# A two-layer hybrid decoder step: pooling gates with their branch products in the attention rounds, the other gates earlier, and a new order inside projections

## The chip, the cores and the metric

The program runs on one core of one Trainium2 chip. The metric is device time in microseconds (us), the median of several executions. Engines are called by the profile's names: PE (TensorE, matmuls), DVE (VectorE), ACT (ScalarE), POOL (GpSimd) and SP (SyncE, which only issues transfers).

## What is computed

Each of two layers takes 256 prompt tokens and 64 sample tokens (8 sequences of 8) of width 1024 through one input projection and three parallel mixers, and merges them under gates:

```
h = xn @ w_in        # pooling input and z, q, kv, rope key, z, conv q/k/v, z, beta, alpha, 3 x 1024 gates
y_a = pool_mixer(h_pool) * silu(z_pool)          # trailing windows of 2, 4, 8, 16
y_b = latent_attention(h_q, h_kv, h_kr) * silu(z_mla)   # samples attend to 2048 cached positions
y_c = rmsnorm(gated_delta(short_conv(h_qkv))) * silu(z_dn)
gates = sigmoid(h_gate)                          # three of 1024
merged = gates[0] * (y_a @ w_br_pool) + gates[1] * (y_b @ w_br_mla) + gates[2] * (y_c @ w_br_dn)
x = x + merged @ w_out
```

After both layers a last RMSNorm is applied. Caches and states are outputs too.

## The kernel before, in words

All activations stand transposed: 128 channels on the partitions, 320 tokens (256 and 64) along them. The width of 1024 makes eight such tiles, and a column block of a weight is a tile of 128 x 1024 (eight blocks of k).

**Products.** Every weight is loaded by SP (`load_w`, four buffers `wraw`) and split in two parts for accuracy: `split_w` has ACT write the rounded part `wh` (line 200) and DVE the rest `wl` (line 201). The numbers in K["lo"] name the splits of a layer whose second part POOL makes instead of DVE. `mm3` (line 213) multiplies with the parts of the activations: for each of eight k, wh by xnH (line 224), wh by xnL (line 225) and wl by xnH (line 226), 24 matmuls into one PSUM bank. A branch product has four k and so 12 matmuls. The first two products of the first layer use another order, both wh products of all k and then all wl products (lines 219 to 221).

**Stages of a layer.** Conv units (`unit`, `value`: a projection, its eviction into V at lines 500 and 501, three steps `cy` at line 509, a gate function) alternate with chunk products of the delta rule; poolings, z projections and latents are fillers that `fill` takes from a list, in the order of K["fo"] and in the numbers that other entries of K give. Then come the inverse of the chunk matrices, the state steps over chunks, eight prompt heads, eight decode rounds (one for each sample sequence, with 2048 cached keys gathered from memory) and the tail: branch products, the merged sum and eight output products. Up to the heads and in the tail a list scheduler puts the instructions of all engines in order; from the heads to the first branch products the order is the program's own (`manual_schedule`) for PE, DVE, ACT and POOL.

**Gates.** There are 24 gate products in a layer, named (n, m): n = 0 for pooling, 1 for the delta rule, 2 for attention, and m one of eight tiles. `gate_w` takes the next of the list `order` and splits its weight, `gate_mm` multiplies, `gate_out` has DVE multiply the bank with the norm (line 464) and ACT take the tanh. Eight (first layer) or seven stand in stages before the heads and stay in SBUF (`early`, 11 buffers `gt`), two among the heads, two in each of six rounds and one in the last two; those 14 are written to memory by ACT's queue and read back in the tail by POOL's. One gate of the second layer stands in the tail.

**A round.** Scores (72 matmuls of four row groups), the largest score and exponent on DVE and ACT, a gate, the combination of the sequence before (`olat`), the first half of the second gate, the turning of the exponents (`PT`, on PE), the other half, and the weighted sum (`pv`). DVE transposes the next keys meanwhile (`flip`).

**Branch products.** `branch_mm` multiplies; `branch_out` multiplies with the gate on DVE (for n = 0 straight into the sum `acc`, line 1358; else line 1360) and has POOL add into the sum (line 1361). In the last round and behind it stand two of the pooling's, two of the delta rule's, then one and two more; the rest follow in the scheduled part. PSUM's four banks "A" serve all of them.

Of the kernel before, what the change touches and what calls it, by code (L numbers as in the profile page):

```python
# [11 lines left out]
F32 = mybir.dt.float32  # L12
# [22 lines left out]
NG = 11  # L35
# [5 lines left out]
KS = [{'kk': [1, 1, 2, 3], 'ga': 3, 'gm': [0, 2, 0], 'un': 16, 'gb': 0, 'gc': [0, 0, 0], 'ft': [5, 2, 3, 3, 2], 'fu': [0, 1, 2, 1], 'fn': 3, 'gs': [0, 0, 2, 1, 0], 'gq': 0, 'gp': [0, 0, 0, 0, 0, 1, 1, 0], 'ge': [1, 1, 1], 'ya': 'B', 'zb': 'A', 'fy': [2, 1, 1], 'fz': [1, 1, 1], 'p1': [2, 2, 2, 2], 'p2': [2, 2, 2, 2], 'hd': [3, 0, 2, 1, 1, 1, 0, 0], 'fo': [0, 1, 2, 3, 4, 5, 6, 7, 8, 9, 12, 13, 10, 14, 11, 18, 15, 16, 17, 19], 'to': [0, 2, 6, 1, 3, 5, 7, 13, 14, 8, 15, 16, 18, 9, 17, 10, 4, 11, 12], 'bt': ['A', 'A', 'A', 'A', 'M'], 'lo': [1, 2, 4, 5, 8, 13], 'zp': [-1, -1, -1, 19, -1, -1, -1, -1], 'f8': 3}, {'kk': [1, 1, 2, 3], 'ga': 3, 'gm': [0, 0, 0], 'un': 8, 'gb': 1, 'gc': [0, 0, 0], 'ft': [5, 2, 3, 3, 1], 'fu': [0, 1, 2, 1], 'fn': 3, 'gs': [0, 0, 2, 1, 0], 'gq': 0, 'gp': [0, 0, 0, 0, 0, 1, 1, 0], 'ge': [1, 1, 2], 'ya': 'B', 'zb': 'B', 'fy': [2, 1, 2], 'fz': [1, 0, 1], 'p1': [2, 2, 3, 1], 'p2': [2, 2, 2, 2], 'hd': [3, 0, 2, 1, 1, 1, 0, 0], 'fo': [0, 1, 5, 2, 3, 4, 6, 7, 8, 9, 12, 13, 10, 14, 11, 18, 15, 16, 17, 19], 'to': [0, 2, 5, 1, 6, 3, 7, 13, 14, 8, 15, 16, 18, 9, 17, 10, 4, 11, 12], 'bt': ['A', 'A', 'A', 'M', 'M'], 'lo': [1, 2, 4, 5, 15], 'zp': [-1, -1, -1, 19, -1, -1, -1, -1], 'f8': 3}]  # L41
LEVELS = (8, 16, 32)

GL, SPILL = (2, 2, 2, 2, 2, 2, 1, 1), 14
# [72 lines left out]
def trunk(tc, I, O, layers=2):  # L117
# [296 lines left out]
    for l in range(layers):  # L414
# [30 lines left out]
        order = [(n, 2 * mp + i) for mp in range(4) for n in range(3) for i in range(2)]  # L445
# [3 lines left out]
        spilled = {}  # L449

        def gate_w(spare=False):
            n, m = order.pop(0)
# [8 lines left out]
        def gate_out(nm, b, spill=False):  # L461

            t = per.tile([128, T], F32, tag="gs" if spill else "gt", name="gt", bufs=2 if spill else NG)
            tt(t, b[:, :T], rn, mult)
            act(t, t, AF.Tanh, scale=0.5)
            if spill:
                spilled[nm] = kept[len(spilled)]
                nc.scalar.dma_start(spilled[nm], t)
            else:
                early[nm] = t  # L470

        def gate(tag, spare=False, spill=False):
            nm, w = gate_w(spare)
            gate_out(nm, gate_mm(tag, w), spill)
# [20 lines left out]
        def conv(ct):  # L495
# [7 lines left out]
            nc.gpsimd.tensor_copy(cnew[:, ct, 0:3], V[:, 256:259])  # L503
            nc.gpsimd.tensor_copy(cnew[:, ct, 3:27].rearrange("p (b j) -> p b j", j=3), Vs[:, :, 8:])
# [30 lines left out]
        def unit(a, p):  # L535
# [6 lines left out]
            nc.gpsimd.tensor_tensor(sq, o, o, mult)  # L542
# [69 lines left out]

        unit(0, 2)
        unit(0, 3)
# [80 lines left out]
        fillers = [fillers[i] for i in K["fo"]]  # L695
        gated = [lambda p=p: zproj(8 + p, C_ZDN + 128 * p) for p in range(4)]
        gated += [lambda i=i: zproj(4 + i, C_ZMLA + 128 * i) for i in range(4)]
        for z, at in zip(gated, K["zp"]):
            if at >= 0:
                fillers.insert(at, z)  # L700
# [310 lines left out]
        fillers += [late[i] for i in K["to"] if not 5 <= i < 13 or K["zp"][i - 5] < 0]  # L1011
# [314 lines left out]
        yb = {}  # L1326

        def split_hi(pool, y0):
            yb[y0] = (pool.tile([128, 4, T], F32R, name=f"yH{y0}"), pool.tile([128, 4, T], F32R, name=f"yL{y0}"))
            for i in range(4):  # L1330
                act(yb[y0][0][:, i, :], zs[y0 + i], AF.Copy)

        def split_lo(y0):
            for i in range(4):
                tt(yb[y0][1][:, i, :], zs[y0 + i], yb[y0][0][:, i, :].bitcast(F32), sub)

        def split_y(pool, y0):
            split_hi(pool, y0)
            split_lo(y0)

# [28 lines left out]
        with tc.manual_schedule(engines={mybir.EngineType.PE, mybir.EngineType.DVE, mybir.EngineType.Activation, mybir.EngineType.Pool}):  # L1369
# [23 lines left out]
            for h in range(11):  # L1393
# [23 lines left out]
                if h == 3:  # L1417
                    gate_out(nm, b, True)
                    b = None
                if h == 8:  # L1420
                    gate_out(nm, b, True)
                    pair[0] = paired[0] = 1
                    gs = [gate_w() for _ in range(GL[0])]
# [10 lines left out]
            for bb in range(NB):  # L1434
                more = bb + 1 < NB
                if not more:
# [3 lines left out]
                    split_hi(p3a, 0)  # L1440
# [167 lines left out]
```

## Time and profile before

| what | value |
|---|---|
| median of three runs | 1044.32 us (1042.73 to 1047.79) |
| profiled execution, its time | 1044.8 us |
| its span, first to last instruction | 1042.8 us |
| mean granted clock of PE | 0.97 of full |
| busy in the span: PE, DVE, ACT, POOL | 987.6, 712.1, 466.5, 332.2 us |
| bytes read and written | 144.17 and 13.68 MB |

Busy time is the time in which an engine ran any of its instructions. Matmuls overlap in their pipeline and their ends are modelled, so PE can be busy without being at its peak; a matmul's price is read from the distance of starts. A mean over the span hides that stretches have different limits, so the rows below are cut by stretch.

### The profile page before, as it was taken

The numbers are of one execution on the slowest core, as the hardware profiler recorded it, in microseconds if no ns is written. First come the engines' busy times: TensorE is split into PE (matmuls) and PEld (weight loads), VectorE is DVE, ScalarE is ACT, GpSimd is POOL, SyncE is SP. The second block draws the span as 40 slices with busy tenths as digits, with TensorE's granted clock in tenths as the row PEclk, the third lists the DMA queues.
The fourth block names the chain that finished last, engine by engine and source line by source line (L and its number), as shares of the span: only waits on it lengthen the run. The fifth ranks groups of instructions, "written<-read, shape, count | busy, mean of one in ns | idle before, by whom it ended". The sixth has DMA issues, their size and how long they took to land.

```text
span 1042.8 us, 24809 instructions
## 1 busy us (share of the span) xinstructions
PE 987.6 (95%) x10211; PEld 865.2 (83%) x10211; DVE 712.1 (68%) x1353; ACT 466.5 (45%) x838; POOL 332.2 (32%) x467
## 2 busy tenths in 40 slices
PE   8988899999999999999989979999999999998996
PEld 6877798997878888789978868999887787877996
DVE  3899974658656666677758988646774675754962
ACT  5554253555443333444546534336455333334453
POOL 3656312124250101035445542221334201100631
PEclk8999899999999999999999989999999999999999
DMA  9533324633656776268563333455256577633861
GB/s 235 158 82 101 96 74 111 184 96 91 203 171 202 242 233 225 78 196 233 144 194 94 86 98 82 109 144 140 71 145 232 163 227 259 189 135 126 237 171 51
DMA packets 202698, 159.22 MB, mean 153 GB/s; under 512 B 27704, under 2 KB 191826, under 8 KB 200010
## 3 DMA queue, kind: packets, MB, share of 16 engines
q1 hardware_dynamic: 176364, 98.47, 34.7%
q0 software_dynamic: 7424, 48.75, 13.2%
q10 hardware_dynamic: 18798, 10.44, 3.5%
q8 instruction: 80, 1.31, 0.5%
q14 instruction: 32, 0.26, 0.1%
HBM read 144.17 MB, written 13.68 MB: 151 GB/s over the span
## 4 chain that ended last, share of the span: by engine, by line
PE 73%; DVE 16%; ACT 5%; issue 3%; DMA 2%; POOL 1%; SPq 0%; DVEq 0%; ACTq 0%; POOLq 0%
PE sc L1186 6%; PE pv L1257 6%; PE pj L224 5%; PE gate L224 5%; PE pj L226 5%; PE pj L225 5%; PE gate L226 5%; PE gate L225 4%; DVE cy L509 4%; DVE wl L201 3%; PE br L226 3%; PE br L224 3%; PE br L225 3%; PE wo L224 2%; PE wo L225 2%
## 5 line engine op out<-in xcount | busy, mean ns | idle before, releaser
L201 DVE TENSOR_TENSOR wl<-wraw,wh 128x1024 fp32r<-128x1024 f32 (+2 forms) x169 | 195.9, 1167 | 83.0 <-ACT wh L200 82.0
L200 ACT ACTIVATE wh<-wraw 128x1024 fp32r<-128x1024 f32 (+1 forms) x180 | 166.5, 935 | 156.4 <-PE pj L225 75.8
L224 PE MATMUL pj<-xnH,wh 128*128 128x320 f32 (+1 forms) x528 | 172.7, 327 | 13.0 <-DVE V L501 7.6
L226 PE MATMUL pj<-xnH,wl 128*128 128x320 f32 (+1 forms) x528 | 170.2, 322 | 6.3 <-DVE wl L201 6.0
L225 PE MATMUL pj<-xnL,wh 128*128 128x320 f32 (+1 forms) x528 | 168.6, 319 | 0.0
L224 PE MATMUL gate<-xnH,wh 128*128 128x320 f32 x384 | 125.4, 326 | 1.7 <-DVE V L501 1.5
L226 PE MATMUL gate<-xnH,wl 128*128 128x320 f32 x384 | 121.2, 316 | 2.2 <-DVE wl L201 1.8
L225 PE MATMUL gate<-xnL,wh 128*128 128x320 f32 x384 | 120.1, 313 | 0.0
L224 PEld LDWEIGHTS pj<-xnH,wh 128*128 128x128 f32 (+1 forms) x528 | 101.8, 193 | 19.0 <-ACT wh L200 7.7
L226 PEld LDWEIGHTS pj<-xnH,wl 128*128 128x128 f32 (+1 forms) x528 | 101.7, 193 | 10.6 <-DVE wl L201 7.9
L225 PEld LDWEIGHTS pj<-xnL,wh 128*128 128x128 f32 (+1 forms) x528 | 101.7, 193 | 4.9 <-issue 3.5
L224 PEld LDWEIGHTS gate<-xnH,wh 128*128 128x128 f32 x384 | 73.4, 191 | 9.3 <-issue 5.7
L1176 DVE STREAM_TRANSPOSE KT<-kv 128x1024 f32<-128x1024 f32 x64 | 78.6, 1228 | 0.5
L226 PEld LDWEIGHTS gate<-xnH,wl 128*128 128x128 f32 x384 | 73.3, 191 | 4.0 <-DVE wl L201 2.6
L225 PEld LDWEIGHTS gate<-xnL,wh 128*128 128x128 f32 x384 | 73.5, 191 | 1.1 <-issue 0.8
L224 PE MATMUL br<-yH,wh 128*128 128x320 f32 x192 | 61.1, 319 | 3.0 <-ACT wh L200 2.6
L226 PE MATMUL br<-yH,wl 128*128 128x320 f32 x192 | 60.4, 316 | 1.8 <-DVE wl L201 1.8
L225 PE MATMUL br<-yL,wh 128*128 128x320 f32 x192 | 60.2, 314 | 0.0
L1186 PE MATMUL sc<-KT,q 32*64 32x256 f32 x2048 | 59.3, 377 | 0.0
L1257 PE MATMUL pv<-kv,PT 128*64 128x256 f32 x512 | 58.8, 382 | 0.2
L509 DVE SCALAR_TENSOR_TENSOR cy<-V,prm,cy 128x344 f32<-128x344 f32 x72 | 56.4, 802 | 0.5
L1186 PEld LDWEIGHTS sc<-KT,q 32*64 32x64 f32 x2048 | 45.8, 131 | 12.0 <-issue 5.7
(410 smaller groups left out, 2045.1 us busy)
## 6 DMA issues: line engine op xcount, KB each, us to landing
wraw<-in_w_in SPq DMA_DIRECT2D x114, 512.0 KB
wraw<-in_w_out SPq DMA_DIRECT2D x16, 512.0 KB
q<-q4d SPq DMA_DIRECT2D x64, 72.0 KB
gate<-gt ACTq DMA_DIRECT2D x28, 160.0 KB
gt<-gate POOLq DMA_DIRECT2D x28, 160.0 KB, 3.5
wraw<-in_w_br_pool SPq DMA_DIRECT2D x16, 256.0 KB
wraw<-in_w_br_dn SPq DMA_DIRECT2D x16, 256.0 KB
wraw<-in_w_br_mla SPq DMA_DIRECT2D x16, 256.0 KB
```

The costliest lines, as they stand in the source:

```text
L200: act(h, raw, AF.Copy)
L201: (nc.gpsimd.tensor_tensor if spare or turn[0] in K["lo"] else tt)(lo, raw, h.bitcast(F32), sub)
L224: nc.tensor.matmul(out, wh[:, k, :], xh[:, first + k, :], start=k == 0, stop=False)
L225: nc.tensor.matmul(out, wh[:, k, :], xl[:, first + k, :], start=False, stop=False)
L226: nc.tensor.matmul(out, wl[:, k, :], xh[:, first + k, :], start=False, stop=k == nk - 1)
L509: stt(y, V[:, j : j + 344], wj(j), y, mult, add)
L1176: nc.vector.transpose(v[:, a], kv[:, a * 1024 : a * 1024 + 1024].rearrange("p (i k c) -> p i k c", i=4, k=8))
L1186: nc.tensor.matmul(sc[64 * hf : 64 * hf + 64, g, :256], q4[r, k, :], krT[r, keys_] if k == 8 else KT[r, k, keys_], start=k == 0, stop=k == 8,)
L1257: nc.tensor.matmul(pv[64 * hf : 64 * hf + 64, :256], PT[:, n * 128 + 64 * hf : n * 128 + 64 * hf + 64], kv[:, r : r + 256], start=n == 0, ...
```

## The change

Four things are done at once.

1. The eight pooling gates leave the list `order`. Round bb computes gate (0, bb) and the branch product (0, bb); the product of both, `sums[bb]`, is written to memory (`first_sum`). The splits of the pooling's activations (`split_y(p2, 0)`) go ahead of the rounds.
2. The other sixteen gates stand ahead of the rounds: 14 in stages before the heads (K["g0"], five places -1 in K["fo"] and K["gm"], K["gc"], K["gs"], K["gq"], K["ga"]), two among the heads. All are written to memory; three buffers `gs` hold them on the way. Three of the z projections move ahead in K["fo"] too.
3. `branch_out` loads the gate, and for the first product of a tile also the pooling's sum, on POOL's queue (six buffers `gt`, four `acc`). The tail has the delta rule's and the attention's products alone.
4. `mm3` takes the order "all wh products, then all wl products" wherever eight k are multiplied and no range of k is given. K["lo"] is empty: DVE makes every second part. The squares of a unit go from POOL to ACT, and ACT makes one copy of the last conv columns (`cnew`) where POOL made two.

```diff
-NG = 11
+NG = 6
-KS = [{'kk': [1, 1, 2, 3], 'ga': 3, 'gm': [0, 2, 0], 'gc': [0, 0, 0], 'gs': [0, 0, 2, 1, 0], 'gq': 0, 'lo': [1, 2, 4, 5, 8, 13],
+KS = [{'kk': [2, 1, 3, 4], 'ga': 1, 'gm': [1, 1, 0], 'gc': [0, 1, 0], 'gs': [0, 1, 1, 1, 0], 'gq': 2, 'lo': [], 'g0': [1, 1],
...
-'fo': [0, 1, 2, 3, 4, 5, 6, 7, 8, 9, 12, 13, 10, 14, 11, 18, 15, 16, 17, 19],
+'fo': [0, -1, 1, 2, -1, 3, 4, -1, 5, 6, 20, 18, 19, 7, 21, 8, 12, 9, 13, 10, 14, 11, 15, 22, 16, 17],
...
-GL, SPILL = (2, 2, 2, 2, 2, 2, 1, 1), 14
+SPILL = 16
...
     def mm3(out, w, x, nk, first=0, ks=None):
-        if l == 0 and turn[0] <= WLP:
+        if nk == 8 and not ks:
...
-        order = [(n, 2 * mp + i) for mp in range(4) for n in range(3) for i in range(2)]
+        order = [(n, 2 * mp + i) for mp in range(4) for n in (1, 2) for i in range(2)]
+        sums = [tc.dram_tile([128, T], F32, name=f"sum{l}_{m}") for m in range(8)]
...
         def gate_mm(tag, w, b=None, ks=(0, 8)):
             b = b or ps(tag, "gate")
             mm3(b[:, :T], w, xn, 8, ks=ks)
...
+        def gate_out(nm, b):
+            t = per.tile([128, T], F32, tag="gs", name="gt", bufs=3)
             tt(t, b[:, :T], rn, mult)
             act(t, t, AF.Tanh, scale=0.5)
-            if spill:
+            if nm[0]:
                 spilled[nm] = kept[len(spilled)]
                 nc.scalar.dma_start(spilled[nm], t)
...
-            nc.gpsimd.tensor_copy(cnew[:, ct, 0:3], V[:, 256:259])
-            nc.gpsimd.tensor_copy(cnew[:, ct, 3:27].rearrange("p (b j) -> p b j", j=3), Vs[:, :, 8:])
+            act(cnew[:, ct, 0:27].rearrange("p (b j) -> p b j", j=3), last3, AF.Copy)
...
-            nc.gpsimd.tensor_tensor(sq, o, o, mult)
+            act(sq, o, AF.Square)
...
         def branch_out(n, m, b):
+            t = per.tile([128, T], F32, tag="gt", name="gt", bufs=NG)
+            nc.gpsimd.dma_start(t, spilled[n, m])
+            if m not in accs:
                 accs[m] = p3a.tile([128, T], F32, tag="acc", name="acc", bufs=4)
+                nc.gpsimd.dma_start(accs[m], sums[m])
+            stt(t, t, 1.0, b[:, :T], add, mult)
+            nc.gpsimd.tensor_tensor(accs[m], accs[m], t, add)
+
+        def first_sum(m, t, b):
+            stt(t, t, 1.0, b[:, :T], add, mult)
+            nc.scalar.dma_start(sums[m], t)
...
-                g = [(gs[0][0], gate_mm("A", gs[0][1]))]
+                (nm, w), w0 = gs
+                g = gate_mm("A", w)
                 if o is not None:
                     ob = combine(o)
                     combined(bb - 1, ob)
-                if two:
-                    b = gate_mm("A", gs[1][1], ks=(0, 4))
                 PT = turned_p(S)
                 PTn = turned_own(bb)
-                    gate_mm("A", gs[1][1], b, (4, 8))
+                b = branch_mm(0, w0, "A")
                 weigh(bb, mx)
                 o = attend(bb, PT, PTn, mx)
+                first_sum(bb, t, b)
```

What the scheduler and the written order make of it is seen in the orders of instructions. Lines in the rows of the change are those of the changed file.

The first place is DVE early in the first layer, among the conv units and the decay terms (`V` is a conv eviction, `cy` a conv step, `al`, `SM`, `t1` the decays, `wl` a weight's second part, `gt` a gate). Before:

```order
L500 TENSOR_TENSOR V_475<-pj_450,rn_112 128x256
L501 TENSOR_TENSOR V_475<-pj_450,rn_112 128x8x8
L201 TENSOR_TENSOR wl_562<-wraw_559,wh_561 128x1024
L582 SCALAR_TENSOR_TENSOR al_405<-al_405,t1_406 8x320
L583 TENSOR_SCALAR al_405<-al_405,adt0_201 8x320
L585 SCALAR_TENSOR_TENSOR SM_399<-cst1_365,al_405 8x320
L500 TENSOR_TENSOR V_527<-pj_502,rn_112 128x256
```

Of the change:

```order
L514 TENSOR_TENSOR V_518<-pj_493,rn_112 128x256
L515 TENSOR_TENSOR V_518<-pj_493,rn_112 128x8x8
L201 TENSOR_TENSOR wl_576<-wraw_573,wh_575 128x1024
L597 SCALAR_TENSOR_TENSOR al_413<-al_413,t1_414 8x320
L598 TENSOR_SCALAR al_413<-al_413,adt0_201 8x320
L600 SCALAR_TENSOR_TENSOR SM_407<-cst1_373,al_413 8x320
L608 TENSOR_TENSOR t1_414<-SM_407 8x256
L609 TENSOR_TENSOR t1_414<-SM_407 8x64
L464 TENSOR_TENSOR gt_569<-gate_544,rn_112 128x320
L524 SCALAR_TENSOR_TENSOR cy_524<-V_518,prm0_197,cy_524 128x344 x2
L201 TENSOR_TENSOR wl_638<-wraw_635,wh_637 128x1024
L524 SCALAR_TENSOR_TENSOR cy_524<-V_518,prm0_197,cy_524 128x344
```

A gate's eviction and its split stand among the conv steps, and a second conv eviction comes later. On PE, up to the first product of the inverse, 552 matmuls of projections and gates stand where 456 stood; up to the first state step 840 for 696, and in the second layer 841 for 673. Eight rounds hold 288 for 348, the tails 383 for 467 and 383 for 491.

The second place is DVE in a middle round (`KT`, `krT` are transposed keys, `olat` the combination, `PTn` the turned own exponents, `S` the scaled scores). Before, from the combination on:

```order
L1273 COPY olat_3363<-olat_4242 128x16x8
L464 TENSOR_TENSOR gt_4246<-gate_4217,rn_112 128x320
L1173 STREAM_TRANSPOSE krT_4209<-kr_4084 128x512
L1176 STREAM_TRANSPOSE KT_4208<-kv_4085 128x4x8x32
L1244 COPY PTn_4279<-PTn_4278 64x64
L464 TENSOR_TENSOR gt_4294<-gate_4252,rn_112 128x320
L1200 COPY mx_3996<-mx_3996 64x1 x2
L1225 TENSOR_TENSOR mx_3996<-mx_3996 128x1
L1226 RECIPROCAL mx_3996<-mx_3996 128x1
L1176 STREAM_TRANSPOSE KT_4208<-kv_4085 128x4x8x32
L201 TENSOR_TENSOR wl_4331<-wraw_4328,wh_4330 128x1024
L201 TENSOR_TENSOR wl_4337<-wraw_4334,wh_4336 128x1024
```

Of the change:

```order
L1292 COPY olat_3589<-olat_4438 128x16x8
L464 TENSOR_TENSOR gt_4442<-gate_4413,rn_112 128x320
L1192 STREAM_TRANSPOSE krT_4405<-kr_4278 128x512
L1195 STREAM_TRANSPOSE KT_4404<-kv_4279 128x4x8x32
L1263 COPY PTn_4461<-PTn_4460 64x64
L1219 COPY mx_4207<-mx_4207 64x1 x2
L1244 TENSOR_TENSOR mx_4207<-mx_4207 128x1
L1245 RECIPROCAL mx_4207<-mx_4207 128x1
L1365 SCALAR_TENSOR_TENSOR gt_4442<-gt_4442,br_4464 128x320
L1195 STREAM_TRANSPOSE KT_4404<-kv_4279 128x4x8x32
L201 TENSOR_TENSOR wl_4512<-wraw_4509,wh_4511 128x1024
L201 TENSOR_TENSOR wl_4518<-wraw_4515,wh_4517 128x512
```

The second gate's eviction has become the product of gate and branch (line 1365), and the second split is half as wide.

The third place is POOL at the start of the first layer's tail (`gt` a gate's load, `acc` a sum and its load, `xT` the load of the layer's input). Before:

```order
L1353 DMA gt_5624<-gate0_2_223 128x320
L1526 DMA xT_5532<-xs0_218 128x2560
L1361 TENSOR_TENSOR acc_5360<-acc_5360,gt_1096 128x320
L1353 DMA gt_5647<-gate0_3_224 128x320
L1361 TENSOR_TENSOR acc_5398<-acc_5398,gt_1704 128x320
L1353 DMA gt_5674<-gate0_4_225 128x320
L1353 DMA gt_5697<-gate0_5_226 128x320
L1361 TENSOR_TENSOR acc_5360<-acc_5360,gt_1738 128x320
L1353 DMA gt_5720<-gate0_6_227 128x320
L1361 TENSOR_TENSOR acc_5398<-acc_5398,gt_2736 128x320
L1353 DMA gt_5743<-gate0_7_228 128x320
L1353 DMA gt_5766<-gate0_8_229 128x320
```

Of the change:

```order
L1356 DMA gt_5545<-gate0_0_221 128x320
L1359 DMA acc_5547<-sum0_0_237 128x320
L1361 TENSOR_TENSOR acc_5547<-acc_5547,gt_5545 128x320
L1356 DMA gt_5578<-gate0_1_222 128x320
L1359 DMA acc_5580<-sum0_1_238 128x320
L1517 DMA xT_5699<-xs0_218 128x2560
L1361 TENSOR_TENSOR acc_5580<-acc_5580,gt_5578 128x320
L1356 DMA gt_5644<-gate0_4_225 128x320
L1359 DMA acc_5646<-sum0_2_239 128x320
L1361 TENSOR_TENSOR acc_5646<-acc_5646,gt_5644 128x320
L1356 DMA gt_5669<-gate0_5_226 128x320
L1359 DMA acc_5671<-sum0_3_240 128x320
```

Before, an add uses a gate that stayed in SBUF or was loaded several rows above; now each add uses the gate of the row or two above it, and the next gate's load stands behind that add. The chain goes on for gates 2 and 3; behind gate 3's load five more loads stand in a row.

## Rows read from the trace of the kernel before

**Rows 1.** Stretches: length, then each engine's busy time (instructions), PE clock, DMA share, GB/s.

```profile
25.00:124.00 99.00, 86.38 (x568) 77.54 (x566) 88.92 (x173) 46.98 (x73) 54.24 (x82) 0.93 0.40 108
124.00:191.30 67.30, 66.06 (x1015) 60.10 (x1014) 43.65 (x81) 27.65 (x43) 16.41 (x25) 1.00 0.37 97
...
313.80:447.50 133.70, 132.20 (x1876) 107.86 (x1876) 87.53 (x171) 49.43 (x95) 14.86 (x28) 1.00 0.60 193
447.50:521.90 74.40, 72.85 (x505) 71.63 (x504) 55.32 (x84) 35.33 (x60) 34.37 (x37) 0.98 0.71 198
521.90:629.70 107.80, 92.28 (x614) 83.40 (x613) 87.33 (x176) 53.35 (x80) 54.16 (x88) 0.92 0.42 118
629.70:694.50 64.80, 63.69 (x1005) 58.20 (x1005) 41.92 (x76) 25.24 (x40) 16.12 (x26) 0.97 0.32 88
...
949.50:1032.00 82.50, 79.09 (x547) 76.85 (x546) 51.25 (x79) 35.94 (x61) 32.45 (x35) 0.98 0.53 154
```

**Rows 2.** Timeline of PE in a round: start, length, line, tile.

```profile
387.20 0.31 PE L225 MATMUL gate<-xnL,wh 128*128 128x320 f32 x1
...
390.43 0.31 PE L226 MATMUL gate<-xnH,wl 128*128 128x320 f32 x1
```

**Rows 3.** PE's groups in 25 to 124: count, busy us, mean ns, idle us before.

```profile
L226 PE MATMUL pj<-xnH,wl 128*128 128x320 f32 (+1 forms) x112 | 37.3, 333 | 2.8 <-DVE wl L201 2.4 <-POOL wl L201 0.3
```

**Rows 4.** DVE's groups over the whole span, by shape.

```profile
L201 DVE TENSOR_TENSOR wl<-wraw,wh 128x1024 fp32r<-128x1024 f32 x119 | 154.4, 1307 | 74.8 <-ACT wh L200 74.4
...
L509 DVE SCALAR_TENSOR_TENSOR cy<-V,prm,cy 128x344 f32<-128x344 f32 x72 | 56.4, 802 | 0.5
...
L464 DVE TENSOR_TENSOR gt<-gate,rn 128x320 f32<-128x320 f32 x48 | 23.2, 483 | 35.3 <-PE gate L226 35.2
...
L642 DVE TENSOR_TENSOR us<-U 128x454 f32<-128x454 f32 x8 | 6.2, 770 | 0.0
```

**Rows 5.** Timelines of POOL and DVE among the conv units, 49 to 73.

```profile
49.60 2.40 POOL L201 TENSOR_TENSOR wl<-wraw,wh 128x1024 fp32r<-128x1024 f32 x1
...
49.96 2.41 DVE L509 SCALAR_TENSOR_TENSOR cy<-V,prm,cy 128x344 f32<-128x344 f32 x1
...
67.65 0.57 DVE L509 SCALAR_TENSOR_TENSOR cy<-V,prm,cy 128x344 f32<-128x344 f32 x1
...
72.19 1.22 DVE L201 TENSOR_TENSOR wl<-wraw,wh 128x1024 fp32r<-128x1024 f32 x1
```

**Rows 6.** POOL's groups over the whole span, by shape.

```profile
L201 POOL TENSOR_TENSOR wl<-wraw,wh 128x1024 fp32r<-128x1024 f32 x11 | 26.6, 2420 | 13.9 <-ACT wh L200 13.8
...
L504 POOL COPY cnew<-V 128x24 f32<-128x24 f32 x24 | 9.8, 409 | 0.0
...
L542 POOL TENSOR_TENSOR sq<-kk 128x320 f32<-128x320 f32 x8 | 7.4, 924 | 0.9 <-DVE kk L520 0.9
```

**Rows 7.** Timeline of PE: turnings of two rounds, and a round with one gate.

```profile
375.60 1.04 PE L1234 MATMUL PT<-cst,S 128*128 128x128 f32 x8
...
392.77 1.03 PE L1234 MATMUL PT<-cst,S 128*128 128x128 f32 x8
...
421.30 0.41 PE L224 MATMUL gate<-xnH,wh 128*128 128x320 f32 x1
...
426.01 1.09 PE L1234 MATMUL PT<-cst,S 128*128 128x128 f32 x8 [0.54 <-ACT S L1216]
...
435.64 0.41 PE L224 MATMUL gate<-xnH,wh 128*128 128x320 f32 x1
```

**Rows 8.** DMA issues: count, KB each, median us from issue to landing.

```profile
gt<-gate POOLq DMA_DIRECT2D x28, 160.0 KB, 3.5
...
xT<-xs POOLq DMA_DIRECT2D x2, 1280.0 KB, 7.0
```

**Rows 9.** Timeline of POOL in the tail: idle time before, and what ended it.

```profile
458.23 0.56 POOL L1353 DMA_DIRECT2D gt<-gate  x1 [0.30 <-POOL acc L1361]
...
480.56 1.31 POOL L1361 TENSOR_TENSOR acc<-acc,gt 128x320 f32<-128x320 f32 x1 [0.45 <-DVE gt L1360]
```

More of the change, by code (lines that the diff above doesn't have):

```diff
@@ L459, in gate_mm, with gate, split_hi, split_lo @@
             return b
-        def gate_out(nm, b, spill=False):
-            t = per.tile([128, T], F32, tag="gs" if spill else "gt", name="gt", bufs=2 if spill else NG)
+        def gate_out(nm, b):
+            t = per.tile([128, T], F32, tag="gs", name="gt", bufs=3)
             tt(t, b[:, :T], rn, mult)
             act(t, t, AF.Tanh, scale=0.5)
-            if spill:
+            if nm[0]:
                 spilled[nm] = kept[len(spilled)]
                 nc.scalar.dma_start(spilled[nm], t)
[L469 to L474, printed above, removed]
+            return t
+        def gate(tag):
+            nm, w = gate_w()
+            gate_out(nm, gate_mm(tag, w))
+        yb = {}
+        def split_hi(pool, y0):
+            yb[y0] = (pool.tile([128, 4, T], F32R, name=f"yH{y0}"), pool.tile([128, 4, T], F32R, name=f"yL{y0}"))
+            for i in range(4):
+                act(yb[y0][0][:, i, :], zs[y0 + i], AF.Copy)
+        def split_lo(y0):
+            for i in range(4):
+                tt(yb[y0][1][:, i, :], zs[y0 + i], yb[y0][0][:, i, :].bitcast(F32), sub)
+        def split_y(pool, y0):
+            split_hi(pool, y0)
+            split_lo(y0)
         rn_s = rn[:, TP:].rearrange("p (b i) -> p b i", i=8)
@@ L611, in trunk @@
         nc.vector.tensor_copy(el4, b[:, :48].rearrange("p (q n) -> p q n", n=12))
+        for _ in range(K["g0"][0]):
+            gate("pj")
         unit(0, 2)
+        for _ in range(K["g0"][1]):
+            gate("pj")
         unit(0, 3)
@@ L694, in trunk @@
         fillers += [lambda i=i: tt(hkv[:, i, :], proj(C_KV + 128 * i), rn, mult) for i in range(2)]
-        fillers = [fillers[i] for i in K["fo"]]
         gated = [lambda p=p: zproj(8 + p, C_ZDN + 128 * p) for p in range(4)]
         gated += [lambda i=i: zproj(4 + i, C_ZMLA + 128 * i) for i in range(4)]
-        for z, at in zip(gated, K["zp"]):
-            if at >= 0:
-                fillers.insert(at, z)
+        fillers = [gated[i - 20] if i >= 20 else fillers[i] if i >= 0 else lambda: gate(chunk.get("tag", "pj")) for i in K["fo"]]
         n_late = len(fillers)
@@ L1010, in trunk @@
         late = [keys, keys_out, queries, transposed_wuk, latent_queries, *gated, *uqs]
-        fillers += [late[i] for i in K["to"] if not 5 <= i < 13 or K["zp"][i - 5] < 0]
+        fillers += [late[i] for i in K["to"] if not 5 <= i < 13 or i + 15 not in K["fo"]]
         pxc = ExitStack()
@@ L1324, in trunk @@
         accs = {}
[L1326 to L1339, printed above, removed]
         def branch_w(n, m):
@@ L1417, in trunk @@
                 if h == 3:
-                    gate_out(nm, b, True)
+                    gate_out(nm, b)
                     b = None
                 if h == 8:
-                    gate_out(nm, b, True)
+                    gate_out(nm, b)
                     pair[0] = paired[0] = 1
-                    gs = [gate_w() for _ in range(GL[0])]
+                    gs = gate_w(nm=(0, 0)), branch_w(0, 0)
                 if h == 9:
@@ L1482, in trunk @@
             wuv = load_wuv(pb.tile([128, 1024], F32, tag="S", name="wuv", bufs=2))
-            branch_out(0, 0, b00)
-            b01 = branch_mm(0, w01, "A")
-            if order:
-                gate("A")
-            w10 = branch_w(1, 0)
+            b10 = branch_mm(1, w10, "A")
             combined(NB - 1, combine(o))
-            b10 = branch_mm(1, w10, "A")
-            branch_out(0, 1, b01)
-            w11 = branch_w(1, 1)
+            b11 = branch_mm(1, w11, "A")
+            branch_out(1, 0, b10)
+            w12 = branch_w(1, 2)
             b = ps("A", "oml")
@@ L1527, in trunk @@
         for mp in range(4):
-            for n in range(3):
+            for n in (1, 2):
                 for m in (2 * mp, 2 * mp + 1):
```

53 lines of the change are left out of this document (18 added, 35 removed).

## Prediction, before the changed kernel was run

> **What bounds the kernel now.** I read the table of stretches first [rows 1], cut where TensorE's (PE's) work changes kind. For each layer it shows the conv units and chunk products (25 to 124, 521.9 to 629.7), called A here; the rest up to the first state step (124 to 191.3, 629.7 to 694.5), called B; the eight decode rounds (313.8 to 447.5, 815.7 to 949.5); and the tail with branch and output products (447.5 to 521.9, 949.5 to 1032). What lies between (state steps, prompt heads) holds as many products after as before and is counted at nothing. The reader is to see two regimes. In rounds, B and tails PE is busy nearly all the time (132.2 of 133.7, 66.1 of 67.3, 72.9 of 74.4) at a granted clock of 0.97 to 1.00: there a product costs its own time. In A, PE is idle 12.6 and 15.5 us and its mean clock is 0.93 and 0.92, while VectorE (DVE) is busy 88.9 of 99.0 and 87.3 of 107.8: there DVE paces the work. The clock has two levels, 2.4 and 1.2 GHz, so a mean of 0.93 is 6.9 us of PE's work lost over 99.0 us, and 0.92 is 8.6 over 107.8.
>
> Next the price of a product. The 2nd and 24th matmul of a gate start 3.23 us apart over 22 steps [rows 2], 0.147 us each: 3.53 us for a product of 24 (projection, gate, output), 1.76 for a branch product of 12.
>
> **The change part by part**, against the profiled execution: 1044.8 us for a span of 1042.8, 0.5 above the median of 1044.32. The program's matmuls of this kind are the same in number; counted in the two orders, what moves is this.
>
> Stretch A gets 96 more in each layer (three gates and, on balance, one projection), 4 x 3.53 = 14.1 us of PE. PE has room for 12.6 + 6.9 = 19.5 in the first layer and 15.5 + 8.6 = 24.1 in the second, if the gaps close and the clock stays up. Of DVE the order shows nine weight splits more in the first layer (three gates, and six that POOL gives back; eight in the second), 1.22 each with no POOL work beside it [rows 5], and nine evictions (three gates, two z of two steps, two latents) of 0.48 [rows 4]: 11.0 + 4.3 and 9.8 + 4.3. Two poolings go behind the mark, with some 20 short steps; their longest take 0.77 [rows 4] and I count 0.35 each, 7.0. DVE's new work is 8.3 and 7.1. Against that stands a relief. A conv step (cy) beside a POOL split of 2.40 took 2.41 us, and alone 0.57 [rows 5]; the mean of its 72 is 0.80 [rows 4], so 36 x 0.23 = 8.3 us a layer are lost beside POOL, and 60 splits x (1.31 - 1.22) = 5.4. The change takes from POOL, per layer, five or six splits of 2.42, 8 squares of about 0.92 and 24 small copies of 0.41 [rows 6], some 30 us, against 54 in A; I take half of the 13.7 back, 6.8. What is left, 1.5 and 0.3, has 10.1 and 20.5 of free time to go to. So A doesn't grow. I take -2 in each layer, because the new order of the projections' products (all with the first weight part, then the second's) also removes waits for the second part (2.8 us of PE's idle time in A before such rows [rows 3]). Bounds: -5.4 and -10 (PE paces, no gaps left), +14.1 each (nothing hidden).
>
> The Trainium skill, "SBUF — State Buffer", section "Who interferes with whom", says that a DVE instruction with two SBUF inputs and a GpSimd one that reads SBUF lock each other out for a whole instruction. The trace agrees (2.41 against 0.57). By that rule alone all the delay that the removed instructions caused would go, up to 13.7 a layer, and the sum would be lower by up to 7 us a layer.
>
> The gates themselves keep the interleaved order: their helper always hands a range of k, so the new path isn't taken and their waits for the second part stay: that half of the change does nothing. ACT gets the squares and one copy for two small ones, POOL's waits there shorten; ACT is busy 47.0 of 99.0, so this is hidden. The weights of the six or seven products that A and B gain, 512 KB each, are loaded where the DMA share is 0.32 to 0.42: hidden too.
>
> Stretch B gets two products in the first layer (7.1) and three in the second (10.6). PE is idle 1.2 and 1.1 there, and the second layer's clock of 0.97 is worth 1.9: +6 and +7.6.
>
> Rounds. Six of eight have two gates, and one lasts 17.17 us (392.77 - 375.60 [rows 7]) without PE idle. After, each has one gate and one branch product, 12 matmuls fewer. But only one gate then stands between the scores and the turning of the softmaxed scores, and those are late: the old seventh round, with one gate, waits 0.54 us for them and lasts 14.34 (421.30 to 435.64). With a branch product put behind the turning (+1.76, less 0.1 of a wait it covers): 16.0. Six rounds gain 1.17, the seventh loses 1.7, the last is unchanged: -5.3 a layer, -10.6. Bounds: -8.8 (60 matmuls, no wait) to +1.7 (rounds don't shorten at all).
>
> Tails. PE loses 84 matmuls in the first layer (12.3 us) and 108 in the second (15.9). I don't give it that. Now every gate comes back from memory, and in the tail's hand-ordered part POOL stands: load gate, load sum, add, load the next gate (the order of POOL above). The load is queued behind an add that needs DVE's step with the gate loaded before; behind that step, on DVE, stand the next products' weight splits, for which PE waits. One turn of that chain: landing 3.5 [rows 8], DVE 0.48 as for a gate's eviction, POOL's wait 0.45, its add 1.31, then 0.30 [rows 9]: 6.0 us. Behind the first product (at about 3 us) stand five turns, so the sixth is at 33 us. The branch products have four PSUM banks, each free only after its DVE step: the tenth product waits for the sixth step. Then 7 x 1.76 and 8 x 3.53: 33 + 12.3 + 28.2 = 73.6 us, against 74.4. In the second layer 2 more for the output's transposes: 75.6 against 82.5. Sum -7.7. Before, loads ran two or three adds ahead and the first eight gates were in SBUF. Bounds: -12.3 and -15.9 (chain hidden), or +17.5 each if every load took the 7.0 of the large one that stands in the same queue [rows 8]. Bytes set no harder limit: 0.71 of the engines at 198 GB/s [rows 1] is 279 at full share, and about 14.5 MB need 52 us.
>
> The Trainium skill, "DMA: Bandwidth & Descriptors", section "Rules for kernel authors", speaks against this part: issue a load early and wait on it late. Its fit in "Anatomy of one DMA" (2.0 us and bytes by 436 GB/s) would give 2.4 for 160 KB, an estimate; the trace has 3.5. By it the sum would be 5.5 a layer lower.
>
> Sum: A -4.0, B +13.6, rounds -10.6, tails -7.7: -8.7, so 1044.8 - 8.7 = **1036 us**.
>
> **The rivals.** *The chain is hidden* (faster). The tails then give their 12.3 + 15.9 = 28.2 instead of 7.7: 1036 - 20.5 = 1016. For it: PE has other products to run meanwhile, and the scheduler has put three output products ahead of the last branch product. Against: POOL's order and four banks.
>
> *DVE can't take it* (slower). DVE's free 10.1 and 20.5 us in A are waits for PE and ACT that stay, and POOL's absence brings it nothing, so its 8.3 and 7.1 us of new work lengthen A in full, where I took -2: 1036 + 10.3 + 9.1 = 1055. It decides once DVE in A is busy above 95%, with PE idle as before. For it: DVE at 90% already. Against: waits for PE's products shrink when the second-part waits go.
>
> *The chain is longer.* Two of its loads stand behind the 1280 KB one and take 7.0 for 3.5, and PE, idle between products, falls to 1.2 GHz, as it does in A: about +6 a layer, 1048.
>
> **How the numbers follow.** A measurement of this kernel tells 0.5%, 5.2 us, from no change: faster is under 1039.1, slower over 1049.5. My sum has 0.44, with 1030 to 1043 as its own range: 0.28 of it faster, 0.16 the same. The hidden chain has 0.25, all faster; DVE 0.18, all slower; the longer chain 0.13, of which 0.02, 0.08 and 0.03. Together 0.55, 0.24, 0.21. The range reaches to both outer cases: 1014 to 1054.
>
> **What would show it.** Right: A as long as before with PE above 90% busy, DVE above it too and the clock near 1; rounds of 16 us with 0.5 us before the turning; in the tail, gate loads on POOL some 6 us apart, five times, each behind an add, and PE idle 2 to 3 us before branch products whose bank a VectorE step frees. Wrong: tails of 62 and 67 us (hidden), or A above 105 and 115 us with DVE full and PE's clock down (DVE). Rounds of 17 us would take back the third term.

## The result, and the profile after

The changed kernel takes 1072.3 us (median of 4 runs, 1070.8 to 1072.9) where the kernel before takes 1043.5 beside it: a ratio of 1.027, 95% interval 1.023 to 1.030. It is slower by 28.8 us between the medians, 27.8 between the two profiled executions; 1036 was forecast, in a range of 1014 to 1054 that doesn't hold the result.

The stretches of the changed kernel's profiled execution, with the columns of [rows 1]: length, busy time (instructions) of PE, its weight loads, DVE, ACT and POOL, clock, DMA share, GB/s. They are in order A, B, what lies between, the rounds and the tail of the first layer, then of the second:

```profile
25.00:122.80 97.80, 93.66 (x659) 87.38 (x658) 87.29 (x174) 57.74 (x98) 23.07 (x41) 0.98 0.51 140
122.80:197.40 74.60, 72.05 (x1050) 66.80 (x1049) 50.34 (x97) 31.71 (x50) 17.02 (x28) 1.00 0.39 105
197.40:325.70 128.30, 121.37 (x1080) 102.51 (x1079) 79.47 (x165) 63.79 (x135) 44.26 (x50) 1.00 0.51 150
325.70:455.10 129.40, 124.82 (x1818) 99.09 (x1816) 83.92 (x170) 43.77 (x87) 14.91 (x28) 1.00 0.58 189
455.10:529.10 74.00, 63.17 (x422) 60.71 (x422) 43.74 (x70) 30.36 (x52) 33.81 (x46) 0.95 0.69 195
529.10:633.60 104.50, 98.03 (x703) 90.83 (x703) 88.39 (x173) 62.49 (x104) 27.74 (x47) 1.00 0.53 147
633.60:712.00 78.40, 75.08 (x1047) 69.62 (x1049) 50.30 (x97) 31.77 (x49) 18.75 (x29) 0.96 0.37 97
712.00:847.60 135.60, 123.85 (x1087) 104.69 (x1083) 75.05 (x162) 63.54 (x136) 40.03 (x50) 0.97 0.48 142
847.60:977.00 129.40, 124.78 (x1817) 99.15 (x1816) 84.03 (x170) 43.74 (x87) 14.93 (x28) 1.00 0.58 189
977.00:1060.30 83.30, 69.83 (x440) 66.91 (x440) 38.52 (x62) 29.98 (x51) 34.45 (x45) 0.88 0.50 146
```

The stretch between state steps and rounds had no row before the prediction, since it was counted at nothing. Here it is, from the kernel before, both layers:

```profile
191.30:313.80 122.50, 119.60 (x1064) 101.49 (x1063) 78.57 (x159) 62.80 (x132) 44.17 (x50) 1.00 0.52 152
694.50:815.70 121.20, 118.61 (x1052) 101.27 (x1051) 77.64 (x158) 62.76 (x131) 41.29 (x48) 1.00 0.51 152
```

Against [rows 1], length after minus length before, first and second layer:

| stretch | forecast | measured | difference |
|---|---|---|---|
| A | -2, -2 | -1.2, -3.3 | -0.5 |
| B | +6, +7.6 | +7.3, +13.6 | +7.3 |
| between | 0, 0 | +5.8, +14.4 | +20.2 |
| rounds | -5.3, -5.3 | -4.3, -4.4 | +1.9 |
| tails | -0.8, -6.9 | -0.4, +0.8 | +8.1 |
| sum | -8.7 | +28.3 | +37.0 |

(The two spans differ by 27.8; what lies behind the last cut is 0.5 shorter.) More than half of the miss is the stretch between, where PE has 16 and 35 instructions more of a thousand, short products of the chunks, and in the second layer is idle for 12 us where it was idle for 3. A single profile tells such a stretch to 1 or 2 us: the run with the tail's loads ahead, below, has the changed kernel's program there and took 129.1 and 135.2. PE's four longest waits there, in the changed kernel, 712 to 815:

```profile
PE ws L1073 <- ACT rs L410: 2.2, 1, 2.2
PE uq L224 <- ACT cqH L206: 2.2, 1, 2.2
PE ss L408 <- POOL sq L405: 1.6, 1, 1.6
PE ckt L951 <- DVE hkv L942: 1.5, 1, 1.5
```

and the only wait shown in the same part of the kernel before, 694.4 to 783:

```profile
PE oT L1111 <- DVE zs L1112: 0.8, 1, 0.8
```

All four belong to one chain: the latents (hkv, hq) are projected, squared on ACT, added on POOL (sq), summed over the partitions by PE (ss), turned into a scale on ACT (rs), multiplied on DVE, split again (cqH), and only then can PE make the first query product (uq). The state step's `ws` takes its PSUM bank from the same set as ss (tag "M") and so waits until rs has read ss. The links of the chain are those of before. Before, three value projections (z) stood beside it; the change made these ahead, moved the fourth there, and put two more gates into this part, but at its end. The number of products is the same and the cover is gone.

The waits cost more than their own time, since the granted clock fell behind them:

```profile
741.00:747.00 6.00, 5.95 (x48) 5.28 (x48) 2.76 (x7) 2.12 (x4) 0.00 (x0) 0.54 0.00 0
```

So of the 14.4 us that the second layer's stretch grew, 9.2 are PE's idle time and about 4 the clock (0.97 over 135.6 us).

In front of this chain ACT itself stands still. Timeline of ACT in the changed kernel (start, length; ACTq are its issues), second layer:

```profile
715.42 6.21 ACTq L1036 DMA_DIRECT2D st<-in_state_delta  x4
721.68 0.38 ACT L1097 ACTIVATE ot<-op 128x256 f32<-128x256 f32 x1 [5.90 <-DMA st<-in_state_delta]
721.96 0.82 ACT L403 ACTIVATE sq<-hkv 128x320 f32<-128x320 f32 x2
```

and in the kernel before:

```profile
695.85 2.96 ACTq L1019 DMA_DIRECT2D st<-in_state_delta  x4
```

The same four issues of 256 KB hold ACT for 6.2 us instead of 3.0, with the latents' squares behind them. So there are two theories: **B**, the cover is gone; **A**, ACT's stall at its queue (the letters of the expectations; the stretches A and B are others). A third difference is that the pooling's splits (`yH`, 1.5 us of ACT) now stand between the squares, in both layers.

The tail's mechanism is as forecast. POOL in the first layer's tail, issues and adds in turn (start, length, idle before and what ended it):

```profile
459.57 0.56 POOL L1356 DMA_DIRECT2D gt<-gate  x1
...
463.12 1.25 POOL L1361 TENSOR_TENSOR acc<-acc,gt 128x320 f32<-128x320 f32 x1 [1.91 <-DVE gt L1360]
464.31 0.57 POOL L1356 DMA_DIRECT2D gt<-gate  x1
...
470.70 1.26 POOL L1361 TENSOR_TENSOR acc<-acc,gt 128x320 f32<-128x320 f32 x1 [5.28 <-DVE gt L1360]
471.90 0.56 POOL L1356 DMA_DIRECT2D gt<-gate  x1
...
477.53 0.56 POOL L1356 DMA_DIRECT2D gt<-gate  x1
...
482.53 3.21 POOL L1356 DMA_DIRECT2D gt<-gate  x6
```

From 459.57 to 482.53 are four turns, 5.7 us each (6.0 forecast), every load behind an add. As forecast, the tenth branch product starts right behind the sixth step on DVE, at 485.64. PE waits for the banks that these steps free, first layer and second:

```profile
PE br L224 <- DVE gt L1360: 8.2, 4, 2.5
...
PE br L224 <- DVE gt L1360: 7.7, 4, 2.5
PE wo L219 <- DVE mgL L210: 2.4, 2, 1.5
PE wo L218 <- ACT mgH L209: 1.4, 1, 1.4
```

What wasn't counted is what stands behind the chain in the second layer. Its tail, cut at the start of the tenth branch product, and two shorter pieces:

```profile
977.00:1008.46 31.46, 21.71 (x145) 19.69 (x145) 13.97 (x28) 8.99 (x17) 13.38 (x21) 0.85 0.65 200
1008.46:1060.30 51.84, 48.12 (x295) 47.22 (x296) 24.54 (x35) 20.99 (x34) 21.07 (x25) 0.89 0.40 114
...
1000.00:1021.00 21.00, 17.67 (x90) 16.92 (x90) 10.43 (x18) 6.83 (x11) 12.45 (x21) 0.70 0.68 192
1021.00:1041.00 20.00, 16.28 (x90) 15.45 (x88) 12.35 (x17) 8.71 (x13) 8.22 (x9) 0.83 0.56 162
```

Up to the cut the chain took 31.5 us of the 33 forecast; behind it stand 51.8 us where 42.5 were forecast. About 6 of the difference is the clock (0.89, partly at 1.2 GHz), and 3.8 are the waits of the output products (wo) for the split of the merged sum, the wo rows above. The whole tail stands at 0.88 where the first layer's is at 0.95.

### The profile page after: what moved, and what is told of

It reads as the page before. It is cut to its first block, busy times and chain, and to the rows that moved or that the text cites. A ratio compares the mean times of both kernels' runs of the same rounds, so it can differ in the third digit from the quotient of the medians.

```text
span 1070.6 us, 24835 instructions
## 1 busy us (share of the span) xinstructions
PE 990.7 (93%) x10211; PEld 866.6 (81%) x10211; DVE 694.4 (65%) x1364; ACT 476.2 (44%) x878; POOL 273.6 (26%) x412
## 3 DMA queue, kind: packets, MB, share of 16 engines
q0 software_dynamic: 8384, 52.03, 13.6%
## 5 line engine op out<-in xcount | busy, mean ns | idle before, releaser
L201 DVE TENSOR_TENSOR wl<-wraw,wh 128x1024 fp32r<-128x1024 f32 (+1 forms) x180 | 199.0, 1117 | 111.9 <-ACT wh L200 110.8
L218 PE MATMUL pj<-xnH,wh 128*128 128x320 f32 (+1 forms) x544 | 170.0, 325 | 11.1 <-DVE gt L464 4.8
L224 PE MATMUL gate<-xnH,wh 128*128 128x320 f32 x384 | 122.4, 319 | 1.8 <-DVE qn L982 1.0
L218 PEld LDWEIGHTS pj<-xnH,wh 128*128 128x128 f32 (+1 forms) x544 | 104.4, 192 | 20.1 <-issue 9.4
L219 PEld LDWEIGHTS pj<-xnL,wh 128*128 128x128 f32 (+1 forms) x544 | 104.6, 192 | 1.4 <-issue 0.3
L221 PE MATMUL pj<-xnH,wl 128*128 128x320 f32 (+1 forms) x544 | 95.6, 314 | 0.0
L221 PEld LDWEIGHTS pj<-xnH,wl 128*128 128x128 f32 (+1 forms) x544 | 83.8, 189 | 2.9 <-issue 2.0
L224 PE MATMUL br<-yH,wh 128*128 128x320 f32 x192 | 65.5, 341 | 15.9 <-DVE gt L1360 15.9
L226 PE MATMUL br<-yH,wl 128*128 128x320 f32 x192 | 62.6, 328 | 3.8 <-DVE wl L201 3.8
L225 PE MATMUL br<-yL,wh 128*128 128x320 f32 x192 | 62.6, 326 | 0.0
L1235 ACT ACTIVATE S<-S,mx 128x1024 f32<-128x1024 f32 x16 | 18.4, 1149 | 84.3 <-DVE mx L1234 72.1
```

The source lines that it names most:

```text
L201: (nc.gpsimd.tensor_tensor if spare or turn[0] in K["lo"] else tt)(lo, raw, h.bitcast(F32), sub)
L1235: act(S, S, AF.Exp, bias=mx[:, 4:5], accum_out=mx[:, 5:6])
```

## The experiments

The medians of the kernel before move a little from one set of runs to the next (1043.5 to 1046.6), so results are compared by their ratio to it; the changed kernel has 1.027.

**The state's loads on SP.**

```diff
-            nc.scalar.dma_start(x, I["state_delta"][l][...])
+            nc.sync.dma_start(x, I["state_delta"][l][...])
```

> The changed kernel with the four loads of the recurrent state (256 KB each, 1024 pieces) issued by SP, not by ACT. In the changed kernel ACT stands 6.2 us at these four issues (3.7 and 4.3 us at the third one alone), in front of the squares of the latents for which PE then waits. Theory A (the stall of ACT at its queue): the stretch from the first state step to the prompt heads, 95.7 and 103.1 us, shrinks by 3 in the first layer and by 6 or more in the second, 1072 -> 1063. Theory B (the cover is gone: projections that stood behind the query latents were moved ahead, so the chain from query latents to the first query product stands bare): the waits of PE before that product stay, each stretch changes by less than 1.5 us, 1070 to 1073.

1066.7 us, ratio 1.018 (1.014 to 1.021). The stretch between:

```profile
198.70:326.30 127.60, 121.45 (x1082) 102.47 (x1081) 79.34 (x165) 63.84 (x135) 43.61 (x50) 1.00 0.52 153
714.00:845.50 131.50, 122.19 (x1093) 103.92 (x1089) 76.32 (x162) 63.54 (x136) 40.09 (x50) 0.97 0.50 147
```

0.7 and 4.1 us less than the changed kernel: the first layer's is as theory B had it, the second's is neither's. There the wait for the squares is gone and the waits for rs and cqH stay, 2.1 and 2.3 us: the stall is a part, and the chain stays bare. In the second layer the scheduler, which orders what isn't ordered by hand, also put one query projection ahead of the sum over the latents, so not all of the 4.1 is the stall's.

**Gates beside the latents.** The number of gates behind each of the five state steps, in both layers:

```diff
-'gs': [0, 1, 1, 1, 0]
+'gs': [2, 1, 0, 0, 0]
```

> The changed kernel with the three gates of the state steps put behind the first and second step (2, 1, 0, 0) instead of one each behind the second to fourth (0, 1, 1, 1): the same products, two of them one place earlier, beside the chain of the latents. Theory B (lost cover): PE's waits before the query products (1.2 to 2.2 us each) go, the stretch from first state step to heads shrinks by 2 and by 5 or more: 1065. Theory A (ACT's stall): a stall of 4 us is covered by the gate that moves up, too, but the waits of the first state step (1.0 us for a first weight part, 1.6 us for a square) stay and the later steps get bare places: -2 to +2, 1070 to 1074.

1059.2 us, ratio 1.011 (1.008 to 1.015).

```profile
197.80:324.70 126.90, 121.37 (x1084) 102.38 (x1083) 81.07 (x165) 62.76 (x135) 41.88 (x50) 1.00 0.51 151
711.80:837.50 125.70, 120.96 (x1090) 102.64 (x1085) 79.06 (x162) 63.62 (x136) 40.28 (x50) 1.00 0.52 154
```

The stretches shrink by 1.4 and 9.9 us (2 and 5 or more expected), and the second layer's clock there is back at 1.00. The waits for rs and cqH are gone from its list; one of 1.7 for a latent's square stays, behind ACT's stall. Theory B holds for most of it: two gates one place earlier, with nothing else moved, take back some 11 us of the 20.

**The tail's loads ahead.** The first six gates and four sums are loaded at the start of the last round:

```diff
+                else:
+                    for nm in ((1, 0), (1, 1), (1, 2), (1, 3), (2, 0), (2, 1)):
+                        ahead_g[nm] = gate_back(*nm)
+                        if nm[0] == 1:
+                            sum_back(nm[1])
...
-            nc.gpsimd.dma_start(t, spilled[n, m])
+            t = ahead_g.pop((n, m), None)
+            if t is None:
+                t = gate_back(n, m)
```

> The changed kernel with the first six gates and first four sums of the tail loaded at the start of the last round, not one by one between the adds. Theory (the chain on POOL sets the tail): PE's idle time in the tails, 10.8 and 13.5 us, falls to 3 in each, the mean clock in the second layer's tail goes from 0.87 to 0.97, the tails shrink by 7 and 15 us: 1050. Rival (the four PSUM banks and VectorE's weight splits set it): idle falls by 3 in each, 1066.

1050.2 us, ratio 1.002 (0.999 to 1.005), and the tails:

```profile
452.80:515.40 62.60, 59.88 (x420) 57.80 (x421) 46.62 (x70) 30.28 (x52) 30.32 (x38) 1.00 0.74 210
966.40:1035.90 69.50, 64.43 (x440) 62.36 (x440) 41.40 (x62) 29.88 (x51) 31.49 (x37) 0.95 0.53 156
```

11.4 and 13.8 us less, PE's idle time 2.7 and 5.1 where it was 10.8 and 13.5, the clock 1.00 and 0.95: the chain of load, add, load set the tails, and that is now shown. The rounds, where the loads now stand, are as long as in the changed kernel (133.7 and 133.5 us from the first scores to the output product of the latents, 133.55 there).

**The old order of products in projections.**

```diff
-        if nk == 8 and not ks:
+        if l == 0 and turn[0] <= WLP:
```

> The changed kernel with the old order of products in projections (first part by both halves of x, then second part, k by k) everywhere it was before. Theory as in the prediction (the new order removes waits for the second weight part): PE idle in the stretches up to the first state step grows by 2 to 4 us a layer, 1072 -> 1078. Rival (the order only moves the wait, since the second part comes on time or the next product waits instead): within 2 us, 1070 to 1074.

1073.3 us, ratio 1.023 (1.018 to 1.028): no difference from the changed kernel, where 1078 was the theory's. In the first layer A and B end 3.0 us later than in the changed kernel's profile (200.4 for 197.4), but that is no more than profiles of one program differ by there (see A below). That the new order keeps A short is not shown.

**Gates and tail together.**

> The changed kernel with both edits of the two runs that gained: gates behind the latents, and tail loads ahead. Theory (two separate places, the gains add): 1072.3 - 13.1 - 22.2 = 1037, faster than before by 6 to 8. Rival (the gains overlap, since the second layer's clock was lost to both): 1043, no gain over before.

1040.3 us, ratio 0.995 (0.993 to 0.996): faster than before by some 5 us (4 to 7), which rules out the rival's 1043. The gains add up all but a few us; the second layer's stretch between is 128.1 here, where the gates alone, with the same program there, had 125.7:

```profile
193.60:320.00 126.40, 121.33 (x1080) 102.34 (x1079) 81.04 (x165) 62.72 (x135) 41.85 (x50) 1.00 0.52 152
700.10:828.20 128.10, 121.17 (x1087) 102.59 (x1081) 77.60 (x162) 63.47 (x136) 40.30 (x50) 1.00 0.50 151
```

**The state's loads on SP as well.**

> The kernel with gates behind the latents and tail loads ahead, and the state's loads issued by SP besides. Theory B (the bare chain was the cause, ACT's stall only one of its links): with the cover back the stall is hidden, within 2 us of that kernel, 1035 to 1039. Theory A (the stall itself costs): 3 to 5 less, 1033.

1035.6 us, ratio 0.991 (0.989 to 0.993). The time is in theory B's range, the ratio is 4 us better than the last one's, as theory A had it, and the intervals meet at their edges. In the trace the first layer's stretch gains 2.2 us and the second's 0.6:

```profile
196.00:320.20 124.20, 120.97 (x1080) 102.34 (x1079) 79.35 (x165) 63.20 (x135) 41.70 (x50) 1.00 0.52 154
697.50:825.00 127.50, 122.10 (x1087) 103.94 (x1081) 78.72 (x162) 63.38 (x136) 39.72 (x50) 0.99 0.51 151
```

So the stall isn't all hidden by the cover, as theory B had it; it is worth some 2 us in the first layer. In the second, where profiles of one program differ by 2.4 (125.7 and 128.1 above), its share is not settled.

**POOL makes second parts again** (with gates and tail as above; the list "lo" of before in place of the empty one).

> The kernel with gates behind the latents and tail loads ahead, and POOL makes the second parts of six and five weights again, as before the change. Theory as in the prediction (POOL's splits delay VectorE's own steps, so taking them away brings back half of 13.7 us a layer against 6 x 1.22 of new work): about even, within 3 us, 1034 to 1040; the mean conv step is 0.05 to 0.2 us longer. Rival (VectorE is full in the conv stretch, 53.1 of 54.0 us in the second layer, and each split that it is spared counts): the stretches up to the first state step shrink by 3 or more a layer, 1031. Rival (the lock costs more than the work): 1043.

1041.2 us, ratio 0.996 (0.994 to 0.998), beside 0.995: even, as the prediction's balance had it. The price is seen in the conv steps on DVE, in the kernel with gates and tail and then here (count, busy, mean ns):

```profile
L524 DVE SCALAR_TENSOR_TENSOR cy<-V,prm,cy 128x344 f32<-128x344 f32 x72 | 49.1, 695 | 2.4 <-ACT cy L522 1.8
```

```profile
L524 DVE SCALAR_TENSOR_TENSOR cy<-V,prm,cy 128x344 f32<-128x344 f32 x72 | 53.2, 748 | 3.4 <-ACT cy L522 2.4
```

DVE's own splits hardly change, 1311 and 1327 ns.

**Whole gates in the new order** (with gates and tail as above).

```diff
-            mm3(b[:, :T], w, xn, 8, ks=ks)
+            mm3(b[:, :T], w, xn, 8, ks=None if ks == (0, 8) else ks)
```

> The kernel with gates behind the latents and tail loads ahead, and the whole gates too take the new order of products, which the changed kernel's gates never reach. From the run with the old order in projections (1073.3 against 1072.3): no difference, 1035 to 1039. Rival (in rounds each gate stands right behind its weights, and a late second part would cost there): rounds shorter by 0.2 us each, 1034.

1038.4 us, ratio 0.991 (0.989 to 0.993) beside 0.995 (0.993 to 0.996). It looks like a small gain that these runs don't settle. It isn't in the rounds: in the second layer they take 133.54 us, from the first scores to the output product of the latents, and 133.55 without it, so the rival's reason falls.

**The kernel before, without the cover.** Three z projections ahead, the fourth in their place:

```diff
-'zp': [-1, -1, -1, 19, -1, -1, -1, -1]
+'zp': [10, 14, 18, -1, -1, -1, -1, -1]
```

> The kernel before with one edit: three value projections (z) that stood beside the state steps are made ahead, and a fourth stands there instead, as in the changed kernel; nothing else is taken over, and no gate fills the places. The stretch from first state step to heads (90.1 and 88.8 us) loses two products, 7.1 us of PE. Theory B (cover): it shrinks by no more than 4 us in a layer, PE idles 3 us or more in it instead of 1.4 and 0.8, and the time rises by 2 to 8 since the stretches ahead get the two products: 1048 to 1054. Rival (the chain of latents has cover enough without them): it shrinks by 6 to 7 us, idle as before, 1040 to 1046.

1084.6 us, ratio 1.037 (1.032 to 1.042), far over both, so the time itself decides nothing. The first layer is the clean reading, from the first state step to the heads, the kernel before and then this one:

```profile
191.30:281.40 90.10, 88.61 (x892) 77.86 (x892) 61.34 (x120) 46.92 (x80) 28.29 (x29) 1.00 0.50 136
```

```profile
205.40:296.30 90.90, 84.86 (x812) 70.82 (x812) 54.99 (x109) 43.96 (x74) 24.55 (x26) 1.00 0.39 103
```

80 matmuls less (48 of them the two products, 7.1 us; the other 32 are short ones of the chunks), and the stretch is 0.8 us longer, with PE idle 6.0 us where it was idle 1.5. Two of its waits, and the same two in the changed kernel's first layer:

```profile
PE us L1063 <- ACT rs L410: 1.3, 1, 1.3
...
PE uq L224 <- ACT cqH L206: 1.0, 1, 1.0
```

```profile
PE us L1080 <- ACT rs L410: 1.3, 1, 1.3
...
PE uq L224 <- ACT cqH L206: 1.0, 1, 1.0
```

This bears theory B out from the other side, and without any gate, spill or new order, nor the pooling's splits between the squares. The time as a whole says more than was asked: A and B of the first layer grow by 14 us for two products. In the second layer the scheduler put four products more behind the first state step than the edit alone would, so that layer is no reading of the cover. Why the two products cost twice their time ahead stays open.

**Half of the branch product ahead of the turning** (with gates, tail and the state's loads as above).

```diff
+                b = branch_mm(0, w0, "A", None, (0, 2))
                 PT = turned_p(S)
                 PTn = turned_own(bb)
-                b = branch_mm(0, w0, "A")
+                branch_mm(0, w0, "A", b, (2, 4))
```

> The kernel with gates behind the latents, tail loads ahead and the state's loads on SP, and in each round half of the branch product (6 of 12 matmuls, 0.88 us) stands before the turning of the softmaxed scores, half behind it. Theory (the second gate that stood there covered the softmax, and PE now waits 0.53 us for it in every round): rounds 16.1 -> 15.6 us, 1035.6 - 16 x 0.53 = 1027. Rival (the wait only moves behind the turning, to the copies of the turned scores on ACT): 1034 to 1037.

1024.3 us, ratio 0.978 (0.974 to 0.983). In the changed kernel each round waits before the turning, as in the timeline of PE:

```profile
368.01 1.09 PE L1253 MATMUL PT<-cst,S 128*128 128x128 f32 x8 [0.53 <-ACT S L1235]
...
384.12 1.09 PE L1253 MATMUL PT<-cst,S 128*128 128x128 f32 x8 [0.54 <-ACT S L1235]
```

16.11 us from one to the next. With half of the product ahead the rounds lose it: PE is busy 124.30 of 124.80 us, and the stretch was 129.40 in the changed kernel. So the wait did not move behind the turning, as the rival had it. The two layers give 9.2 us, where 8.5 were expected:

```profile
322.10:446.90 124.80, 124.30 (x1818) 99.16 (x1817) 83.22 (x170) 44.42 (x87) 19.10 (x36) 1.00 0.63 206
```

**And whole gates in the new order.**

> As the run with half of the branch product ahead, and the whole gates in the new order of products besides. From the run that had this order alone (1038.4 against 1040.3, intervals that overlap): within 3 us of that run, 1024 to 1030.

1020.6 us, ratio 0.975 (0.970 to 0.980), below the expected range and within the last one's interval. This version is faster than the kernel before by 2.5% and than the changed one by about 5%.

## Why the prediction was wrong

**The step that failed most** is the first cut: what lies between "holds as many products after as before and is counted at nothing". The count was right. But which product stands beside which wait had changed, and a stretch in which PE is busy 119.6 of 122.5 us was taken as one without waits, when its waits were all covered. It cost 20 of the 37 us. The two gates moved back beside the chain take back some 11 of them, and the kernel before with the z projections taken away gets the same waits; ACT's stall at its queue adds to it.

**A** was right as far as the profiles resolve it: -1.2 and -3.3 for -2 each, with PE at 93.7 of 97.8 us and 98.0 of 104.5. But the profiles of the changed kernel and of the six experiments that leave A alone end it at 118.9 to 124.0 us in the first layer: 2 us are within that spread, while the 8.3 that the rival "DVE can't take it" adds are not. DVE's busy time hardly changed (87.3 for 88.9, 88.4 for 87.3), as the balance of relief and new work said, and DVE stayed at 89% and 85%, where it was to be above 90. The conv step's mean fell from 802 to 694 ns, 36 x 0.108 = 3.9 us a layer, where half of 8.3 was taken; POOL's splits given back return half of that, 695 to 748. The reason given for the -2, the new order of products, is not borne out: without it, A is as long within what the runs tell.

**B** was right in the first layer (7.3 for 6) and half of it in the second (13.6 for 7.6). There 3.0 us of idle time and clock were to be won; the clock fell from 0.97 to 0.96 and PE's idle time grew. The gaps of a busy stretch were taken as room, and new products did not go into them.

**Rounds**: 16.11 us for 16.0, with the wait of some 0.5 us that was forecast in front of the turning: 13 of them in the profile, 8.6 us together, the first of a layer up to 1.4.

**Tails**: the first layer's came out at 74.0 for 73.6 by the chain as forecast, though so close by luck: the tenth branch product stood at 30.5 us and not at 33, and what lies behind it took 43.5 and not 40.5. In the second layer the chain was the same and the time 83.3 for 75.6: the terms that were missing are the clock behind the tenth product, about 6 us, and the output products' waits for the merged sum, 3.8. The rival "the chain is longer" had the fall of the clock in it, but at 6 us a layer together with late loads, and in both layers; the chain itself was not longer. The experiment that takes the chain away confirms the ceiling that the hidden-chain rival gave: its tails of 62 and 67 us came out at 62.6 and 69.5, though not in this change.

**"DVE can't take it"** fell: DVE is busy 89% of the first layer's A and 85% of the second's, not above 95 (in one part, 586 to 640, it is busy 53.1 of 54.0 us), and sparing it eleven splits brought nothing.

The sum was on the wrong side although four of the five terms in the first layer stood within 1.3 us, because the fifth was never priced.

## What to carry to other kernels

When a change moves work ahead, price both places: where it goes, by the room there, and where it came from, by the latency that it covered. A stretch with PE busy 98% may be full of waits that only the moved work hides; look for the chain through other engines under it before counting equal numbers of products as equal time. And loads that are issued between the steps that use them form a chain of their own; where buffers are free earlier, issue them there.

## What the runs showed of the hardware

Four loads of 256 KB in 1024 pieces each, issued by ACT, held it for 3.0 us in one kernel and 6.2 in another, 4.3 us of that at one issue, while ACT's next activation waited 5.9 us; an engine that issues such loads can stand still in its own work. What fills the queue then was not tried.

With four waits of PE of 1.7 to 2.5 us between products the granted clock was 0.79 over 15 us in the first layer's tail (475 to 490), and 0.70 and 0.83 over 41 us in the second's, with nearly the same waits: 0.95 and 0.88 over the two tails. What makes the difference is open. In one piece of 6 us behind two waits of 2.2 it was 0.54, nearly all at 1.2 GHz.

The mean granted clock of a whole run moves with no change of the program, and the time with it: over ten runs of the kernel with the tail's loads ahead, from 0.982 at 1042.0 us to 0.971 at 1052.2.
